# Two-layer hybrid decoder trunk on one core: the SBUF tiles of the matmul operands are given other addresses

## The chip, the core and the metric

One core of one Trainium2 chip runs the whole program in one launch. The metric is the device time of one execution in microseconds (us), from the profiler of the chip. TensorE does the matmuls, VectorE (DVE) and ScalarE (ACT) the element-wise work, GpSimd (POOL) some small vector work, and SyncE (SP) issues the DMAs. All weights are float32 and come from HBM once per execution.

## What is computed

Two layers over 256 positions with a model width of 2048. In each layer a normalised input goes through one input projection (2048 to 2816 columns), whose columns feed three mixers: sliding-window attention, a diagonal complex state-space model and a gated MLP over positions. Their outputs are normalised, concatenated and sent through an output projection (2048 to 2048). Then comes a SwiGLU feed-forward block with an inner width of 5632. Cut to the large products:

```python
for l in range(DEPTH):                       # DEPTH = 2
    h = rmsnorm(x, norm_mix[l])
    z = h @ w_in[l]                          # 256x2048 @ 2048x2816
    q, k, v, u_ssm, z_u, z_v = split(z)
    y = concat([rmsnorm(sliding_window_gqa(q, k, v)),
                rmsnorm(s5_mixer(u_ssm)),    # has one 512x512 product inside
                rmsnorm(gmlp_mixer(z_u, z_v))])
    x = x + y @ w_out[l]                     # 256x2048 @ 2048x2048
    h = rmsnorm(x, norm_ffn[l])
    x = x + (silu(h @ w_gate[l]) * (h @ w_up[l])) @ w_down[l]   # 2048x5632 twice, 5632x2048
return rmsnorm(x, norm_final)
```

## The kernel before

**Split products.** A float32 product is made of three products of a faster float32 form (float32r): each operand is split into a rounded high part and the low rest, and high times high, high times low and low times high are summed in PSUM. The function `unit` (L254 to L262) issues them: for one block of 128 input channels `k` and for each of the two halves `m` of the 256 positions, L260 multiplies the high activations with `whi`, L261 the high activations with `wlo`, and L262 the low activations with `whi`. The activations are the stationary operand (128 x 128, loaded into the array before each matmul), and the weights are the moving operand (128 x 512, streamed through). So each matmul has its own weight load, and the stationary operand changes place twice in each group of three.

**Stationary tiles.** `xh` and `xl` hold the transposed, normalised residual stream, high and low part: 16 blocks of 256 columns each. They serve the input projection and the gate and up products. `ya` and `yb` serve the output projection and the down product: `ya` holds blocks 0 to 7 (first high, then low part), `yb` blocks 8 to 15. In the profile a matmul is named by its moving and its stationary tile, in this order: `acc<-whi,xh`.

**Moving tiles.** The weights come in "halves" of 128 x 1024 floats, 512 KB each. `pump` (a DMA per half into one of 5 `raw` buffers), `split_hi` (ACT copies `raw` to `whi`, L168) and `split_lo` (DVE subtracts, `wlo`, L178) prepare them; `whi` and `wlo` have 4 buffers each. One half feeds 12 matmuls of 512 columns. Loads and splits run at most three halves ahead, by the fixed rules of `take_half`.

**Order.** The program order is written by hand: `dense` walks over the blocks, and after each block `tick` lets the side work (attention, state-space model, norms, transposes) issue a few instructions. Nothing in it depends on where a tile lies.

**Addresses.** Before the change there are two SBUF pools, `const` and `work`. A pool lays its tiles one behind the other, in the order of their first allocation, and the second pool begins where the first ends. `xh` and `xl` are allocated in `const` right behind `x`; all others named here are in `work`.

Of the kernel before, what the change touches and what calls it, by code (L numbers as in the profile page):

```python
# [1 line left out]

# [8 lines left out]
F32R = mybir.dt.float32r  # L11
# [107 lines left out]
class Split:  # L119
    def __init__(self, parts):  # L120
        self.parts = parts

    def _at(self, i, k0, k1):
        hi, lo, base = self.parts[k0 // 8 if len(self.parts) > 1 else 0]
        return (hi, lo)[i][:, k0 - base:k1 - base]
# [3 lines left out]

    def lo(self, k0, k1):  # L130
        return self._at(1, k0, k1)


class Builder:
# [811 lines left out]
    def build(self):  # L946
        nc = self.nc
        dr = self.dr
        cst = self.const
        W = self.work  # L950

        self.x = cst.tile([128, 2, 2048], F32, name="x")
        xh = cst.tile([128, 16, 256], F32R, name="xh")
        xl = cst.tile([128, 16, 256], F32R, name="xl")
        self.X = Split([(xh, xl, 0)])
        self.Y = Split([None, None])
        self.ident = cst.tile([128, 128], F32, name="ident")
# [50 lines left out]
        for l in range(L):  # L1008
# [53 lines left out]
            for t in out_tiles():  # L1062
# [12 lines left out]
                f = n not in accs  # L1075
# [80 lines left out]
        for m in range(2):  # L1156
            r = nrm["rs"][:, m:m + 1]
            t = self.work.tile([128, 2], F32, tag="ms", name="ms", bufs=4)
# [13 lines left out]
def build_program(shapes):  # L1172
    nc = bacc.Bacc("TRN2", target_bir_lowering=False, num_devices=1, dynamic_dma_scratch_size=1024)
    dr = {n: nc.dram_tensor(n, s, F32, kind="ExternalInput").ap() for n, s in shapes.items()}
    dr["out"] = nc.dram_tensor("out", (2, 128, D), F32, kind="ExternalOutput").ap()
    with tile.TileContext(nc) as tc:
        with tc.tile_pool(name="const", bufs=1) as cst, tc.tile_pool(name="work", bufs=1) as wrk, \
                tc.tile_pool(name="ps", bufs=1, space=bass.MemoryType.PSUM) as ps, \
                tc.tile_pool(name="dram", bufs=1, space=bass.MemoryType.DRAM) as dram:
            with tc.manual_schedule():  # L1180
                b = Builder(nc, tc, (cst, wrk, ps, dram), dr)
                b.build()
    return nc, b

# [11 lines left out]
```

## Time and profile before

| what | value |
|---|---|
| median of 3 runs | 2106.04 us (2104.9 to 2107.2) |
| the profiled execution: its own time | 2106.98 us |
| its span, first to last instruction | 2105.1 us |
| mean granted TensorE clock | 0.994 of 2.4 GHz |
| TensorE matmuls: busy, number | 2076.0 us, 99% of the span, 9728 |
| weight loads: busy | 1708.8 us, 81% |
| VectorE busy | 1213.1 us, 58% |
| ScalarE busy | 969.4 us, 46% |
| DMA | 387.98 MB, 184 GB/s on average |

The page counts an engine busy from the start to the (modelled) end of each instruction. Matmuls are pipelined: each is on record for some 390 ns and the next one starts some 230 ns after it, so the busy time of TensorE does not tell how fast it works. The distance from one start to the next does.

### The profile page before, as it was taken

To read this page: it belongs to the slowest core of one execution; us is meant where nothing else is said; L and a number is where in the kernel's file an instruction comes from. 1 tells how busy PE (TensorE), PEld (TensorE's weight loads), DVE (VectorE), ACT (ScalarE), POOL (GpSimd) and SP (SyncE) were. 2 spreads that over 40 slices of the span, in tenths; PEclk is the share of its full clock that TensorE was granted. 3 is DMA by queue.
4 is the path that set the end of the run, shared out by engine and by line. 5 is a ranking of instruction groups with operands and counts; after the bars stand their busy time and mean duration, and the time that the engine had idled before them with its cause. 6 is when DMAs were issued, how large, how long until landed. Compare 5 with 4: busy or idle time off the path is not lost.

```text
span 2105.1 us, 25614 instructions
## 1 busy us (share of the span) xinstructions
PE 2076.0 (99%) x9728; PEld 1708.8 (81%) x9728; DVE 1213.1 (58%) x1625; ACT 969.4 (46%) x1289; POOL 204.4 (10%) x196
## 2 busy tenths in 40 slices
PE   8998999999999999999999999999999999999998
PEld 7788888888888888888888888888888888888886
DVE  6998765655555555444556795554454444554445
ACT  6555554444444443344455445544443444434443
POOL 0555004031312100000000010000000000000000
PEclk9998999999999999999999999999999999999999
DMA  7433455565656565555565455555555555555554
GB/s 243 166 128 133 140 180 190 185 212 189 220 189 214 185 210 190 190 183 188 180 215 179 152 187 174 180 189 181 188 183 191 187 184 186 187 191 183 187 193 140
DMA packets 105595, 387.98 MB, mean 184 GB/s; under 512 B 12288, under 2 KB 13056, under 8 KB 104192
## 3 DMA queue, kind: packets, MB, share of 16 engines
q1 hardware_dynamic: 105472, 386.35, 54.8%
q8 instruction: 76, 1.25, 0.2%
q14 instruction: 47, 0.39, 0.1%
HBM read 375.03 MB, written 11.27 MB: 184 GB/s over the span
## 4 chain that ended last, share of the span: by engine, by line
PE 95%; DVE 3%; issue 1%; ACT 0%; DMA 0%; SPq 0%; POOLq 0%; POOL 0%; ACTq 0%
PE acc L260 29%; PE acc L261 29%; PE acc L262 29%; PE side L324 2%; PE side L834 1%; DVE wlo L178 1%; PE side L606 1%; PE side L798 1%; DVE st L614 0%; PE side L566 0%; PE side L823 0%; PE side L644 0%; PE side L642 0%; PE side L639 0%; DMA x<-x 0%
## 5 line engine op out<-in xcount | busy, mean ns | idle before, releaser
L178 DVE TENSOR_TENSOR wlo<-raw,whi 128x1024 fp32r<-128x1024 f32 (+1 forms) x687 | 857.5, 1253 | 686.9 <-ACT whi L168 685.7
L168 ACT ACTIVATE whi<-raw 128x1024 fp32r<-128x1024 f32 (+1 forms) x687 | 725.3, 1057 | 1005.5 <-PE acc L262 943.8
L260 PE MATMUL acc<-whi,xh 128*128 128x512 f32 (+1 forms) x1792 | 711.4, 397 | 1.4 <-ACT whi L168 1.4
L261 PE MATMUL acc<-wlo,xh 128*128 128x512 f32 (+1 forms) x1792 | 701.6, 392 | 0.2 <-DVE wlo L178 0.2
L262 PE MATMUL acc<-whi,xl 128*128 128x512 f32 (+1 forms) x1792 | 701.3, 391 | 0.0
L262 PEld LDWEIGHTS acc<-whi,xl 128*128 128x128 f32 x1792 | 337.5, 188 | 77.4
L260 PEld LDWEIGHTS acc<-whi,xh 128*128 128x128 f32 x1792 | 337.9, 189 | 73.5 <-ACT whi L168 1.8
L261 PEld LDWEIGHTS acc<-wlo,xh 128*128 128x128 f32 x1792 | 338.0, 189 | 73.0 <-DVE wlo L178 1.0
L260 PE MATMUL acc<-whi,ya 128*128 128x512 f32 x512 | 204.6, 400 | 0.0
L262 PE MATMUL acc<-whi,ya 128*128 128x512 f32 x512 | 202.0, 395 | 0.0
L261 PE MATMUL acc<-wlo,ya 128*128 128x512 f32 x512 | 202.0, 394 | 0.0
L260 PE MATMUL acc<-whi,yb 128*128 128x512 f32 x448 | 176.6, 394 | 0.0
L262 PE MATMUL acc<-whi,yb 128*128 128x512 f32 x448 | 174.8, 390 | 0.0
L261 PE MATMUL acc<-wlo,yb 128*128 128x512 f32 x448 | 174.5, 390 | 0.0
L298 POOL TENSOR_TENSOR rs<-ms,nh 128x2 f32<-128x2 f32 (+1 forms) x12 | 12.2, 1014 | 1532.9 <-DVE ms L297 1413.6
L262 PEld LDWEIGHTS acc<-whi,ya 128*128 128x128 f32 x512 | 96.3, 188 | 22.7
L261 PEld LDWEIGHTS acc<-wlo,ya 128*128 128x128 f32 x512 | 96.5, 189 | 21.5
L260 PEld LDWEIGHTS acc<-whi,ya 128*128 128x128 f32 x512 | 96.5, 189 | 21.3
L262 PEld LDWEIGHTS acc<-whi,yb 128*128 128x128 f32 x448 | 84.1, 188 | 18.0
L260 PEld LDWEIGHTS acc<-whi,yb 128*128 128x128 f32 x448 | 84.1, 188 | 17.1
L261 PEld LDWEIGHTS acc<-wlo,yb 128*128 128x128 f32 x448 | 84.2, 188 | 17.0
L360 DVE SCALAR_TENSOR_TENSOR xl<-side,gains,xh 128x256 fp32r<-128x256 f32 x64 | 27.9, 479 | 45.6 <-ACT xh L358 45.5
(223 smaller groups left out, 1278.0 us busy)
## 6 DMA issues: line engine op xcount, KB each, us to landing
raw<-wts SPq DMA_DIRECT2D x684, 512.0 KB, 3.8
saved<-stash SPq DMA_DIRECT2D x4, 1792.0 KB, 6.5
stash<-saved SPq DMA_DIRECT2D x3, 1792.0 KB, 7.4
stashb<-saved SPq DMA_DIRECT2D x2, 1792.0 KB, 9.4
bc<-bc SPq DMA_DIRECT2D x8, 256.0 KB, 3.5
out<-x SPq DMA_DIRECT2D x8, 256.0 KB, 3.0
saved<-stashb SPq DMA_DIRECT2D x1, 1792.0 KB, 7.4
x<-x SPq DMA_DIRECT2D x3, 512.0 KB, 8.0
```

Of the source, the lines that this page charges most:

```text
L168: self.nc.scalar.activation(out=h[:, o:o + w], in_=self.raw[j][:, o:o + w], func=AF.Copy)
L178: self.nc.vector.tensor_tensor(out=o[:, i:i + w], in0=r[:, i:i + w], in1=self.hi[j][:, i:i + w], op=ALU.subtract)
L260: nc.tensor.matmul(out=o, lhsT=a, rhs=wh, start=first, stop=False)
L261: nc.tensor.matmul(out=o, lhsT=a, rhs=wl, start=False, stop=False)
L262: nc.tensor.matmul(out=o, lhsT=b, rhs=wh, start=False, stop=last)
L298: nc.gpsimd.tensor_tensor(out=out, in0=t, in1=self.nh[:, 0:w], op=ALU.pow)
L324: nc.tensor.transpose(ps[:, 256 * kk + 128 * m:256 * kk + 128 * m + 128], parts(2 * b + kk, m), self.ident)
L360: nc.vector.scalar_tensor_tensor(out=o, in0=src, scalar=gain[:, k:k + 1], in1=h.bitcast(F32), op0=ALU.mult, op1=ALU.subtract)
L606: nc.tensor.matmul(out=ps[:, 256 * o + 64 * g:256 * o + 64 * g + 64], lhsT=st[nm][:, 128 * g:128 * g + 128], rhs=U4[:, 4 * ct + g, :])
L798: nc.tensor.matmul(out=ps[:, nk * i:nk * i + nk], lhsT=qT[:, h0 + i], rhs=self.kT[:, j, cq, 0:nk], start=(j == 0), stop=(j == 1))
L834: nc.tensor.matmul(out=ps[:, 64 * i:64 * i + 64], lhsT=pT[:, 128 * (nb * i + b):128 * (nb * i + b) + 128], rhs=self.v[:, b, 64 * cq:64 * c ...
```

## The change

`xh` and `xl` move from the pool `const` into the class `Homes`, which stands in place of the one pool `work`. It holds three pools, one behind the other in SBUF, and sends each tag to one of them: tags that are named nowhere to the first, `whi`, `wlo`, `xh` and `xl` to the second, `ya` and `yb` to the third. Numbers and sizes of the buffers stay as they are. On each engine the same instructions stand in the same order with the same waits; only addresses differ.

```diff
+class Homes:
+    TAGS = (
+        (),
+        ('whi', 'wlo', 'xh', 'xl'),
+        ('ya', 'yb'),
+    )
+    def __init__(self, pools):
+        self.home = {t: p for ts, p in zip(self.TAGS, pools) for t in ts}
+        self.rest = pools[0]
+    def tile(self, shape, dtype, tag, name, bufs=1):
+        return self.home.get(tag, self.rest).tile(shape, dtype, tag=tag, name=name, bufs=bufs)
...
-        xh = cst.tile([128, 16, 256], F32R, name="xh")
-        xl = cst.tile([128, 16, 256], F32R, name="xl")
+        xh = W.tile([128, 16, 256], F32R, tag="xh", name="xh")
+        xl = W.tile([128, 16, 256], F32R, tag="xl", name="xl")
...
-        with tc.tile_pool(name="const", bufs=1) as cst, tc.tile_pool(name="work", bufs=1) as wrk, \
...
+            cst = pool("const")
+            homes = Homes([pool(f"work{i}") for i in range(len(Homes.TAGS))])
...
-                b = Builder(nc, tc, (cst, wrk, ps, dram), dr)
+                b = Builder(nc, tc, (cst, homes, ps, dram), dr)
```

Where the tiles lie in each partition, in KiB from the start of SBUF (from the two built programs):

| tile | size | before | after |
|---|---|---|---|
| `x` (residual stream, float32) | 16 | 1.125 to 17.125 | 1.125 to 17.125 |
| `xh`, `xl` (stationary) | 16 each | 17.125 to 49.125 | 127.75 to 159.75 |
| `raw`, 5 buffers | 20 | 56.625 to 76.625 | 24.625 to 44.625 |
| `whi`, 4 buffers (moving) | 16 | 78.75 to 94.75 | 159.75 to 175.75 |
| `wlo`, 4 buffers (moving) | 16 | 94.75 to 110.75 | 175.75 to 191.75 |
| `t4`, 4 buffers (side work) | 16 | 110.75 to 126.75 | 46.75 to 62.75 |
| `qT`, `kT` (attention) | 8, 4 | 134.875 to 142.875, 143.875 to 147.875 | 70.875 to 78.875, 79.875 to 83.875 |
| `yb` (stationary) | 16 | 148.0 to 164.0 | 191.75 to 207.75 |
| `ya` (stationary) | 16 | 197.375 to 213.375 | 207.75 to 223.75 |

## Rows read from the trace of the kernel before

**Rows 1.** The page: span, then busy time, share and instructions by engine

```profile
span 2105.1 us, 25614 instructions
PE 2076.0 (99%) x9728; PEld 1708.8 (81%) x9728; DVE 1213.1 (58%) x1625; ACT 969.4 (46%) x1289; POOL 204.4 (10%) x196
```

**Rows 2.** The page: chain that ended last, shares of the span by engine

```profile
PE 95%; DVE 3%; issue 1%; ACT 0%; DMA 0%; SPq 0%; POOLq 0%; POOL 0%; ACTq 0%
```

**Rows 3.** Waits of TensorE: waiting line, releaser, total us, times, longest us

```profile
PE side L324 <- DMA x<-x: 6.7, 2, 4.6
PE side L834 <- DVE pT L829: 5.9, 4, 2.3
...
PE acc L260 <- ACT whi L168: 1.4, 1, 1.4
```

**Rows 4.** Groups by form: moving,stationary, shape, count | busy us, mean ns | idle

```profile
L260 PE MATMUL acc<-whi,xh 128*128 128x512 f32 x1728 | 693.1, 401 | 1.4 <-ACT whi L168 1.4
L261 PE MATMUL acc<-wlo,xh 128*128 128x512 f32 x1728 | 683.5, 396 | 0.2 <-DVE wlo L178 0.2
L262 PE MATMUL acc<-whi,xl 128*128 128x512 f32 x1728 | 683.2, 395 | 0.0
L260 PE MATMUL acc<-whi,ya 128*128 128x512 f32 x512 | 204.6, 400 | 0.0
L262 PE MATMUL acc<-whi,ya 128*128 128x512 f32 x512 | 202.0, 395 | 0.0
L261 PE MATMUL acc<-wlo,ya 128*128 128x512 f32 x512 | 202.0, 394 | 0.0
L260 PE MATMUL acc<-whi,yb 128*128 128x512 f32 x448 | 176.6, 394 | 0.0
L262 PE MATMUL acc<-whi,yb 128*128 128x512 f32 x448 | 174.8, 390 | 0.0
L261 PE MATMUL acc<-wlo,yb 128*128 128x512 f32 x448 | 174.5, 390 | 0.0
```

**Rows 5.** Timeline, down product of layer 2: start us, duration us, instruction; yb, then ya

```profile
1838.24 0.39 PE L261 MATMUL acc<-wlo,yb 128*128 128x512 f32 x1
...
1847.76 0.39 PE L261 MATMUL acc<-wlo,yb 128*128 128x512 f32 x1
...
1848.22 0.40 PE L260 MATMUL acc<-whi,ya 128*128 128x512 f32 x1
...
1859.14 0.40 PE L262 MATMUL acc<-whi,ya 128*128 128x512 f32 x1
```

**Rows 6.** Timeline, gate and up products of layer 1

```profile
1000.15 0.39 PE L261 MATMUL acc<-wlo,xh 128*128 128x512 f32 x1
...
1008.09 0.39 PE L262 MATMUL acc<-whi,xl 128*128 128x512 f32 x1
```

**Rows 7.** Groups by form: the matmuls of 256 columns, main and attention

```profile
L260 PE MATMUL acc<-whi,xh 128*128 128x256 f32 x64 | 18.3, 286 | 0.0
L262 PE MATMUL acc<-whi,xl 128*128 128x256 f32 x64 | 18.1, 283 | 0.0
L261 PE MATMUL acc<-wlo,xh 128*128 128x256 f32 x64 | 18.1, 282 | 0.0
...
L798 PE MATMUL side<-kT,qT 128*128 128x256 f32 x64 | 10.4, 290 | 0.0
```

**Rows 8.** Windows: stretch, busy us (count) by engine, clock, DMA share, GB/s

```profile
0.00:200.00 200.00, 180.19 (x1022) 153.74 (x1022) 169.09 (x377) 119.99 (x232) 81.41 (x88) 0.98 0.51 175
...
1470.00:2105.00 635.00, 625.80 (x2737) 507.57 (x2735) 313.37 (x295) 258.96 (x273) 1.79 (x2) 1.00 0.55 183
```

**Rows 9.** The page: the two splits of a weight half, and its DMA

```profile
L178 DVE TENSOR_TENSOR wlo<-raw,whi 128x1024 fp32r<-128x1024 f32 (+1 forms) x687 | 857.5, 1253 | 686.9 <-ACT whi L168 685.7
L168 ACT ACTIVATE whi<-raw 128x1024 fp32r<-128x1024 f32 (+1 forms) x687 | 725.3, 1057 | 1005.5 <-PE acc L262 943.8
...
raw<-wts SPq DMA_DIRECT2D x684, 512.0 KB, 3.8
```

More of the change, by code (lines that the diff above doesn't have):

```diff
@@ L1 @@
+import contextlib
 import math
@@ L1176, in build_program @@
     with tile.TileContext(nc) as tc:
-        with tc.tile_pool(name="const", bufs=1) as cst, tc.tile_pool(name="work", bufs=1) as wrk, \
-                tc.tile_pool(name="ps", bufs=1, space=bass.MemoryType.PSUM) as ps, \
-                tc.tile_pool(name="dram", bufs=1, space=bass.MemoryType.DRAM) as dram:
+        with contextlib.ExitStack() as st:
+            pool = lambda name, **kw: st.enter_context(tc.tile_pool(name=name, bufs=1, **kw))
+            cst = pool("const")
+            homes = Homes([pool(f"work{i}") for i in range(len(Homes.TAGS))])
+            ps = pool("ps", space=bass.MemoryType.PSUM)
+            dram = pool("dram", space=bass.MemoryType.DRAM)
             with tc.manual_schedule():
-                b = Builder(nc, tc, (cst, wrk, ps, dram), dr)
+                b = Builder(nc, tc, (cst, homes, ps, dram), dr)
                 b.build()
```

## The prediction, made before the changed kernel ran

> **What bounds the kernel now.** I read the page from the top first: TensorE is busy for 99% of the span [rows 1] and carries 95% of the chain that ended last [rows 2]. The waits of TensorE come to little: the longest entry is 6.7 us at the start, and the splits of the weights hold it up for about 1.4 us [rows 3]. So nobody feeds TensorE late; what counts is how fast it gets through its own matmuls. A change of addresses alone can touch the time only there, or by making another engine slow enough to be waited for.
>
> The second view is the timeline, read by distances between starts. With `yb` as stationary tile, 42 matmuls in a row take 1847.76 - 1838.24 = 9.52 us, which is 226.7 ns each; with `ya`, in the same down product right behind it, 47 take 1859.14 - 1848.22 = 10.92 us, 232.3 ns each [rows 5]. With `xh` and `xl`, 34 take 1008.09 - 1000.15 = 7.94 us, 233.5 ns each [rows 6]. All three stretches have the same shape, the same moving buffers, the granted clock at the 2.4 GHz level, and no waits. At that clock 512 columns need 213.3 ns if one column goes in per cycle, so every matmul pays 13 to 20 ns on top, and how much depends on which stationary tile it has.
>
> The third view, the groups by form, shows that this isn't a chance of three stretches. Over all matmuls of 512 columns the mean durations are 401, 396 and 395 ns for `xh`, `xh` and `xl` at L260, L261 and L262, 400, 394 and 395 ns for `ya`, and 394, 390 and 390 ns for `yb` [rows 4]. The differences, 7, 6 and 5 ns between `xh`/`xl` and `yb`, are those of the timeline. What the three tiles differ in is the address: `xh` and `xl` lie between 17 and 49 KiB, `ya` between 197 and 213, `yb` between 148 and 164, and `whi` and `wlo` always between 79 and 111.
>
> **The change part by part.** No instruction is added, removed or moved, and no queue is passed; the sum has only paces in it.
>
> *Residual tiles.* `xh` and `xl` go to 127.75 to 159.75 KiB, almost on the place where `yb` was. I give them its pace: 1728 x (401 - 394) + 1728 x (396 - 390) + 1728 x (395 - 390) ns = 12.1 + 10.4 + 8.6 = 31.1 us less [rows 4]. The other bound is 0, if the place was not what made `yb` fast. The 192 matmuls of 256 columns I leave at 0: they are 0.2 us per ns.
>
> *Branch tiles.* `yb` goes to 191.75 to 207.75 KiB, where `ya` was for most of that stretch. I give it `ya`'s pace: 448 x (6 + 5 + 4) ns = 6.7 us more, and 0.2 us for its 48 further matmuls in the state-space branch, so 6.9 us more [rows 4]. The other bound is 0. `ya` stays at the top and keeps its pace; its other bound is `yb`'s pace, 512 x (6 + 5 + 4) ns = 7.7 us less.
>
> *Weight tiles.* `whi` and `wlo` go from 79-111 to 160-192 KiB. The trace has no dense matmul with its moving tile elsewhere, so this cost is unknown on both sides. The only matmuls of some length with both operands between 128 and 192 KiB are those of attention, `kT` with `qT`, 256 columns: 290 ns on average, against 282 to 286 for the main matmuls of the same shape [rows 7]. The 290 also has pauses between heads in it. So the nearest row shows neither a gain nor a clear loss, and I take 0. For the bounds I use one more step of the size that the trace does show, 6 ns per matmul either way: over 3 x (1728 + 512 + 448) + 48 = 8112 matmuls that is 49 us.
>
> *Splits, transposes and DMAs* read and write other addresses too. Their cost is taken as 0, since TensorE covers them: a half feeds 12 matmuls, 12 x 233 ns = 2.80 us, in which DVE needs 1.25 us and ACT 1.06 us for it [rows 9], and at 12 x 227 ns = 2.72 us that still fits. The DMA engines are busy for 0.55 of the last stretch and would be for 0.57 [rows 8]. The cover is thinnest in the first 200 us, where DVE is busy for 169 us [rows 8]: if the whole gain were lost there, it would be at most 1022 x 6 ns = 6 us, which goes into the range.
>
> The sum is -31.1 + 6.9 = -24.2 us. The profiled execution took 2106.98 us, 0.9 above the median of the runs and 1.9 above its own span, so both are one state; 2106.98 - 24.2 = 2082.8, and from the median 2106.04 the forecast is 2082 us.
>
> **The rivals.**
>
> *Alignment, not region.* `yb` starts at 148.0 KiB, a multiple of 256 bytes; `xh` at 17.125 and `ya` at 197.375 KiB are both 128 bytes off one. Each stationary block is 512 bytes long in its partition, so it touches two pieces of 256 bytes if aligned and three if not, and the extra 13.3 and 20 ns stand just as 2 to 3. In the new layout all four tiles begin at such a multiple. Then `xh`, `xl` and `ya` all get `yb`'s pace and `yb` keeps it: -31.1 - 7.7 = -38.8, about 2067 us. Against it: the attention tile `qT` is 128 bytes off too, and its matmuls show no special price [rows 7].
>
> *The moving place counts as well, in the good direction.* One more step of 6 ns for all: -49 on the forecast, about 2033 us. Nothing in the trace shows a main matmul below 226 ns.
>
> *Place is irrelevant.* The paces may belong to the stage and not to the tile; then nothing changes, 2106 us. Against it: `ya` and `yb` differ within one and the same down product, with the same side work around [rows 5]. The Trainium skill speaks for this case: "TensorE: Matmul & The Clock Gate", in its step-by-step part, has the two operands on independent SBUF read ports, so that a weight load takes no bandwidth from the running matmul, and it gives some 216 ns from start to start at 512 columns. "SBUF — State Buffer", under who interferes with whom, says that TensorE never waits for anyone there. The trace differs from these pages: 226.7, 232.3 and 233.5 ns.
>
> *The pace belongs to the pair (slower).* `yb` may have been fast since it lay in another 64 KiB range than its moving tile and at the right distance from it, and not by its own place. The change puts `xh` and `xl` beside `whi` and `wlo` in one range, so they stay at 233 ns, and `yb` loses its distance: +6.9, 2113 us. It is slower as soon as less than 6.9 of the 31.1 us of the residual tiles come.
>
> *Both operands collide in one range (slower).* If a weight load and a stream out of the same 64 KiB hinder each other more than now, each `xh` and `xl` matmul grows by a further step of 6 ns, 5184 x 6 = 31 us, `ya`, next to them, by 9, and `yb` by 2 steps, 17: +57, about 2163 us. For it is only the 290 against 283 ns of [rows 7].
>
> **How the numbers follow.** Chances: forecast 0.34; alignment 0.20; moving place good 0.09; irrelevant 0.12; pair 0.15; collision 0.10. The predicted time is the forecast's, 2082. The range from 2062 to 2116 holds forecast, alignment, irrelevant and pair with 2 to 5 us around, 0.81 together; it leaves out the two unknown extremes, 2033 and 2163. A measurement of this kernel can tell about 0.2%, 4 us, from no change. Faster: 0.34 + 0.20 + 0.09 = 0.63. Same: 0.12. Slower: 0.15 + 0.10 = 0.25.
>
> **What would show it.** In the trace of after, the groups `acc<-whi,xh`, `acc<-wlo,xh` and `acc<-whi,xl` should show means of 394, 390 and 390 ns, and a stretch of the timeline 227 ns from start to start. The `yb` groups should go up to 400, 394 and 395; if they stay at 394, 390 and 390 and `ya` comes down to them, it is alignment. Means below 390 would say that the moving place counts. `xh` at 401 with `yb` at 400 is the pair, and `xh` above 405 the collision. DVE and ACT means of 1253 and 1057 ns should stay, and TensorE's waits should stay below 25 us in all; waits for `whi` or `wlo` that grow by 10 us or more would make the sum wrong in a way that none of the cases holds.

## The result, and the profile after

The changed kernel takes 2071.38 us (2070.53 to 2073.31, 4 runs) against 2106.27 us for the kernel before, measured beside it. The ratio is 0.9836, with a 95% interval from 0.9819 to 0.9853: 34.9 us less. The forecast was 2082 us, 24 less, from 2062 to 2116. The sign and the range held, but the forecast gave the gain to a wrong cause, charged `yb` with a loss that did not come and missed the gain of `ya`, as the rows show.

The page of the changed kernel, the lines that answer to [rows 1] and [rows 2]:

```profile
span 2068.7 us, 25614 instructions
PE 2040.8 (99%) x9728; PEld 1707.3 (83%) x9728; DVE 1210.8 (59%) x1625; ACT 969.7 (47%) x1289; POOL 207.0 (10%) x196
...
PE 95%; DVE 3%; issue 1%; ACT 0%; DMA 0%; SPq 0%; POOLq 0%; POOL 0%; ACTq 0%
```

TensorE bounds the kernel as before, with the same instructions. Its busy time fell by 35.2 us, the span by 36.4; VectorE and ScalarE do their work in the same time (1210.8 and 969.7 us, before 1213.1 and 969.4). So it is the matmuls that got faster. Which of them, the groups by form tell (line, moving and stationary tile, shape, count, then busy us and the mean ns of one; the line numbers are 18 higher than before):

```profile
L278 PE MATMUL acc<-whi,xh 128*128 128x512 f32 x1728 | 685.7, 397 | 1.8 <-ACT whi L186 1.8
L280 PE MATMUL acc<-whi,xl 128*128 128x512 f32 x1728 | 675.5, 391 | 0.0
L279 PE MATMUL acc<-wlo,xh 128*128 128x512 f32 x1728 | 674.9, 391 | 0.4 <-DVE wlo L196 0.4
L278 PE MATMUL acc<-whi,ya 128*128 128x512 f32 x512 | 202.0, 394 | 0.0
L280 PE MATMUL acc<-whi,ya 128*128 128x512 f32 x512 | 199.6, 390 | 0.0
L279 PE MATMUL acc<-wlo,ya 128*128 128x512 f32 x512 | 199.4, 389 | 0.0
L278 PE MATMUL acc<-whi,yb 128*128 128x512 f32 x448 | 176.4, 394 | 0.0
L280 PE MATMUL acc<-whi,yb 128*128 128x512 f32 x448 | 174.6, 390 | 0.0
L279 PE MATMUL acc<-wlo,yb 128*128 128x512 f32 x448 | 174.4, 389 | 0.0
```

Against [rows 4]: `xh` and `xl` came down by 4 to 5 ns, `ya` came down by 5 to 6 ns to the values of `yb`, and `yb` did not go up at all. The timeline says the same in distances between starts, at a granted clock of 1.00 in all these stretches, before and after. First `xh` and `xl` (34 matmuls in 990.39 - 982.68 = 7.71 us, 226.8 ns each, before 233.5 [rows 6]), then `yb` (47 in 10.66 us, 226.8 ns, before 226.7) and `ya` (44 in 9.98 us, 226.8 ns, before 232.3 [rows 5]) in the down product of layer 2:

```profile
982.68 0.39 PE L279 MATMUL acc<-wlo,xh 128*128 128x512 f32 x1
...
990.39 0.39 PE L280 MATMUL acc<-whi,xl 128*128 128x512 f32 x1
...
1806.08 0.39 PE L278 MATMUL acc<-whi,yb 128*128 128x512 f32 x1
...
1816.74 0.39 PE L280 MATMUL acc<-whi,yb 128*128 128x512 f32 x1
1816.96 0.39 PE L278 MATMUL acc<-whi,ya 128*128 128x512 f32 x1
...
1826.94 0.39 PE L280 MATMUL acc<-whi,ya 128*128 128x512 f32 x1
```

All three stretches now have one pace. Over the whole trace, the distances from each start to the next, added up by stationary tile, fell by 26.7 us for `xh` and `xl`, by 8.1 us for `ya` and by 0.6 us for `yb`; 1.0 us of the 36.4 is left for everything else. The prediction said what that would mean: "if they stay at 394, 390 and 390 and `ya` comes down to them, it is alignment". The experiments had to tell which alignment, and whether the 64 KiB ranges (SBUF counted from its start in pieces of 64 KiB) had any share in it.

### The profile page after: what moved, and what is told of

It reads as the page before. It is cut to its first block, busy times and chain, and to the rows that moved or that the text cites. A ratio compares the mean times of both kernels' runs of the same rounds, so it can differ in the third digit from the quotient of the medians.

```text
span 2068.7 us, 25614 instructions
## 1 busy us (share of the span) xinstructions
PE 2040.8 (99%) x9728; PEld 1707.3 (83%) x9728; DVE 1210.8 (59%) x1625; ACT 969.7 (47%) x1289; POOL 207.0 (10%) x196
## 4 chain that ended last, share of the span: by engine, by line
PE 95%; DVE 3%; issue 1%; ACT 0%; DMA 0%; SPq 0%; POOLq 0%; POOL 0%; ACTq 0%
PE acc L278 29%; PE acc L280 29%; PE acc L279 29%; PE side L342 2%; PE side L852 1%; DVE wlo L196 1%; PE side L624 1%; PE side L816 1%; DVE st L632 0%; PE side L584 0%; PE side L841 0%; PE side L662 0%; PE side L660 0%; PE side L657 0%; DMA raw<-wts 0%
## 5 line engine op out<-in xcount | busy, mean ns | idle before, releaser
L196 DVE TENSOR_TENSOR wlo<-raw,whi 128x1024 fp32r<-128x1024 f32 (+1 forms) x687 | 855.2, 1250 | 659.7 <-ACT whi L186 658.9
L186 ACT ACTIVATE whi<-raw 128x1024 fp32r<-128x1024 f32 (+1 forms) x687 | 726.0, 1058 | 972.2 <-PE acc L280 920.8
L278 PE MATMUL acc<-whi,xh 128*128 128x512 f32 (+1 forms) x1792 | 704.0, 393 | 1.8 <-ACT whi L186 1.8
L280 PE MATMUL acc<-whi,xl 128*128 128x512 f32 (+1 forms) x1792 | 693.6, 387 | 0.0
L279 PE MATMUL acc<-wlo,xh 128*128 128x512 f32 (+1 forms) x1792 | 693.0, 387 | 0.4 <-DVE wlo L196 0.4
L280 PEld LDWEIGHTS acc<-whi,xl 128*128 128x128 f32 x1792 | 337.6, 188 | 69.4
L278 PE MATMUL acc<-whi,ya 128*128 128x512 f32 x512 | 202.0, 394 | 0.0
L280 PE MATMUL acc<-whi,ya 128*128 128x512 f32 x512 | 199.6, 390 | 0.0
L280 PE MATMUL acc<-whi,yb 128*128 128x512 f32 x448 | 174.6, 390 | 0.0
L280 PEld LDWEIGHTS acc<-whi,ya 128*128 128x128 f32 x512 | 96.1, 188 | 20.3
L280 PEld LDWEIGHTS acc<-whi,yb 128*128 128x128 f32 x448 | 84.1, 188 | 17.7
```

The lines of the kernel that those rows point to most:

```text
L186: self.nc.scalar.activation(out=h[:, o:o + w], in_=self.raw[j][:, o:o + w], func=AF.Copy)
L196: self.nc.vector.tensor_tensor(out=o[:, i:i + w], in0=r[:, i:i + w], in1=self.hi[j][:, i:i + w], op=ALU.subtract)
L278: nc.tensor.matmul(out=o, lhsT=a, rhs=wh, start=first, stop=False)
L279: nc.tensor.matmul(out=o, lhsT=a, rhs=wl, start=False, stop=False)
L280: nc.tensor.matmul(out=o, lhsT=b, rhs=wh, start=False, stop=last)
```

## The experiments

Three theories were open. **Alignment**: the stationary tile has to begin at a multiple of 256 bytes. **Relative alignment**: it has to be a multiple of 256 bytes away from the moving tile, wherever both are; two tiles at such a distance are called in step below. **Region pair**: 64 KiB ranges count, and a stationary tile is fast in the range of its moving tile or in the next one above; all the places seen so far fit that too. The first four runs were made in one job, beside 2105.26 us for the kernel before. In the profiles of the runs the line numbers are higher by the lines that an edit adds.

### 128 unused bytes ahead of `xh`, in the kernel before

```diff
         self.x = cst.tile([128, 2, 2048], F32, name="x")
+        cst.tile([128, 32], F32, name="pad")
         xh = cst.tile([128, 16, 256], F32R, name="xh")
```

> The kernel before with one unused tile of 128 bytes allocated ahead of xh, and nothing else: every tile behind it moves up by 128 bytes and stays in its old place otherwise (xh 17.25, whi 78.875, yb 148.125, ya 197.5 KiB). Theory alignment (the stationary tile has to begin at a multiple of 256 bytes): xh, xl and ya become aligned and yb falls out of line, so xh, xl and ya come down to 394/390/390 ns and yb goes up to 400/395/394: -29 to -31 -8 +7, about 2075 us. Rival region pair (fast when the stationary tile lies in the same 64 KiB range as the moving one or in the next above): no range changes, 2106 us and the means of before. Rival relative alignment (the distance from stationary to moving tile counts modulo 256 bytes): all tiles move together, 2106 us.

Measured: 2105.96 us, ratio 1.0002 (0.9992 to 1.0011). The groups kept their means; one of each kind:

```profile
L260 PE MATMUL acc<-whi,xh 128*128 128x512 f32 x1728 | 693.1, 401 | 1.4 <-ACT whi L168 1.4
...
L261 PE MATMUL acc<-wlo,ya 128*128 128x512 f32 x512 | 202.0, 394 | 0.0
...
L261 PE MATMUL acc<-wlo,yb 128*128 128x512 f32 x448 | 174.6, 390 | 0.0
```

`xh`, `xl` and `ya` now begin at multiples of 256 bytes and are as slow as before, and `yb` lies 128 bytes off one and is as fast as before. So the tile's own alignment does not count; the alignment rival, as the prediction put it, has fallen. Since everything moved together, the distances did not change.

### 128 unused bytes at the start of the second pool, in the changed kernel

```diff
-        ('whi', 'wlo', 'xh', 'xl'),
+        ('whi', 'wlo', 'xh', 'xl', 'pad', 'pad2'),
...
+        W.tile([128, 32], F32, tag="pad", name="pad")
         xh = W.tile([128, 16, 256], F32R, tag="xh", name="xh")
```

> The changed kernel with an unused tile of 128 bytes at the start of the second pool: xh, xl, whi, wlo, yb and ya all move up by 128 bytes, each in its 64 KiB range. Theory alignment: all stationary tiles fall out of line, 400/395/394 ns for xh, xl, ya and yb, and the time goes back beyond the kernel before: 2071 + 30 + 8 + 7, about 2116 us (2106 if the step is a little smaller than measured). Rival region pair: 2071 us. Rival relative alignment: 2071 us, since stationary and moving tiles move together.

Measured: 2071.42 us, ratio 0.9839 (0.9823 to 0.9856), the changed kernel's own time. It is the counterpart of the first run: all operands are off a multiple of 256 bytes, all distances are as they were, and nothing is lost.

### Only `xh` and `xl` 128 bytes off

```diff
-        ('whi', 'wlo', 'xh', 'xl'),
         ('ya', 'yb'),
+        ('whi', 'wlo'),
+        ('pad', 'xh', 'xl'),
...
+        W.tile([128, 32], F32, tag="pad", name="pad")
         xh = W.tile([128, 16, 256], F32R, tag="xh", name="xh")
```

> The changed kernel with the three groups in another order: ya and yb from 127.75, whi and wlo from 159.75 (where the change puts them), then 128 unused bytes, then xh and xl from 191.875 KiB. Only xh and xl are off a multiple of 256 bytes. Theory alignment: xh and xl at 400/395/394 ns, ya and yb at 394/390/390, 2071 + 30 = about 2101 us. Rival region pair: ya and yb share the range of whi and wlo, xh and xl lie in the next above, so all are fast: 2071 us. Rival relative alignment: as alignment, 2101 us.

Measured: 2097.13 us, ratio 0.9963 (0.9950 to 0.9976), 25.7 us more than the 2071.42 of the run before it, in which all distances are those of the changed kernel. The groups at the first two lines of the three:

```profile
L279 PE MATMUL acc<-whi,xh 128*128 128x512 f32 x1728 | 693.7, 401 | 1.5 <-ACT whi L187 1.5
L280 PE MATMUL acc<-wlo,xh 128*128 128x512 f32 x1728 | 683.6, 396 | 0.6 <-DVE wlo L197 0.6
...
L279 PE MATMUL acc<-whi,ya 128*128 128x512 f32 x512 | 202.0, 395 | 0.0
...
L280 PE MATMUL acc<-wlo,yb 128*128 128x512 f32 x448 | 174.4, 389 | 0.0
```

Exactly the two tiles that are out of step went back to 401 and 396 ns. The region pair has fallen with this: `xh` lies between 192 and 208 KiB with its moving tile between 160 and 192, just where `yb` was fast in the changed kernel, and differs from it by 128 bytes.

### Only `whi` and `wlo` 128 bytes off

```diff
-        ('whi', 'wlo', 'xh', 'xl'),
         ('ya', 'yb'),
+        ('xh', 'xl'),
+        ('pad', 'whi', 'wlo'),
```

(and the same unused tile as above)

> The changed kernel with ya and yb from 127.75, xh and xl from 159.75, then 128 unused bytes, then whi and wlo from 191.875 KiB: only the moving tiles are off a multiple of 256 bytes, and all stationary ones are aligned. Theory alignment of the stationary tile: nothing changes, 2071 us and 394/390/390 ns in all groups. Rival relative alignment: all matmuls slow, about 2116 us. Rival region pair: all stationary tiles lie one range below the moving ones, as xh and xl did before, so all slow: about 2116 us.

Measured: 2114.83 us, ratio 1.0044 (1.0029 to 1.0058). Every stationary tile begins at a multiple of 256 bytes, and every group is slow, `yb` with them. `xh` and `xl` lie at 159.75 to 191.75 KiB here, inside the region from 128 to 192 KiB that the forecast took for fast:

```profile
L279 PE MATMUL acc<-whi,xh 128*128 128x512 f32 x1728 | 693.4, 401 | 1.8 <-ACT whi L187 1.8
...
L280 PE MATMUL acc<-wlo,ya 128*128 128x512 f32 x512 | 202.1, 395 | 0.0
...
L280 PE MATMUL acc<-wlo,yb 128*128 128x512 f32 x448 | 176.9, 395 | 0.0
```

So the same loss comes from moving the other operand. Of the three theories only the relative one fits all four runs.

### 128 unused bytes ahead of `whi`, in the kernel before

A second job (before: 2104.69 us) turned the theory into an edit of the old layout that should help with no tile leaving its range.

```diff
+        if not j:
+            self.work.tile([128, 32], F32, tag="pad", name="pad")
         h = self.work.tile([128, 1024], F32R, tag="whi", name="whi", bufs=self.NH)
```

> The kernel before with 128 unused bytes ahead of whi (the first run put them ahead of xh). xh and xl stay at 17.125 KiB, whi moves to 78.875, yb to 148.125, ya to 197.5 KiB. Theory relative alignment (the matmul is fast when stationary and moving tile are a multiple of 256 bytes apart): xh and xl come into step (61.75 KiB apart) and fall to about 396/391/391 ns, yb stays in step (69.25) at 394/390/390, ya stays out of step (118.625) at 400/395/394: 2105 - 29 = about 2076 us. Rival region pair, or any theory of 64 KiB ranges: no tile changes its range, 2105 us.

Measured: 2079.42 us, ratio 0.9879 (0.9863 to 0.9896), 25.3 us less from 128 bytes that nothing uses.

```profile
L262 PE MATMUL acc<-whi,xh 128*128 128x512 f32 x1728 | 684.7, 396 | 2.2 <-ACT whi L170 2.2
...
L263 PE MATMUL acc<-wlo,ya 128*128 128x512 f32 x512 | 201.9, 394 | 0.0
...
L263 PE MATMUL acc<-wlo,yb 128*128 128x512 f32 x448 | 174.6, 390 | 0.0
```

`xh` came into step (397 or less), `yb` stayed in step and `ya` out of it, each as expected. The first run put the same 128 bytes ahead of `xh`, where they moved both operands, and got nothing.

### Distances of 32 to 224 bytes

Two variants of the changed kernel put `whi` and `wlo` first and unused tiles of 32 to 160 bytes ahead of the stationary tiles (only the order of the tags and the sizes of these tiles differ).

> The changed kernel with whi and wlo first (127.75 KiB), then xh and xl 32 bytes, yb 64 bytes and ya 96 bytes beyond a multiple of 256 from them. Theory pieces of 256 bytes, all or nothing: every distance that isn't 0 costs the full step, all groups at 400/395/394 ns, about 2114 us. Rival graded cost: the step grows from 0 to 128 bytes, so xh and xl lose little (1 to 3 ns, below 2085 us in all), yb about half, ya more. Rival steps of 128 or 64 bytes: groups below the boundary stay at 394/390/390.

> The same with xh and xl 160 bytes, yb 192 and ya 224 bytes beyond a multiple of 256 from whi. All or nothing: all groups at 400/395/394 ns, about 2114 us. Graded: ya nearly at 394/390/390, yb half way, xh and xl most. Steps of 128 bytes: all as at 128, slow; steps of 64: ya differs from the others.

Measured: 2115.89 and 2113.46 us, one run each. One group of each tile, first with `xh` 32, `ya` 96 and `yb` 64 bytes out of step:

```profile
L281 PE MATMUL acc<-wlo,xh 128*128 128x512 f32 x1728 | 684.8, 396 | 0.2 <-DVE wlo L198 0.2
...
L281 PE MATMUL acc<-wlo,ya 128*128 128x512 f32 x512 | 202.9, 396 | 0.0
...
L281 PE MATMUL acc<-wlo,yb 128*128 128x512 f32 x448 | 177.0, 395 | 0.0
```

and then with `xh` 160, `ya` 224 and `yb` 192 bytes out of step:

```profile
L281 PE MATMUL acc<-wlo,xh 128*128 128x512 f32 x1728 | 687.1, 398 | 0.6 <-DVE wlo L198 0.6
...
L281 PE MATMUL acc<-wlo,ya 128*128 128x512 f32 x512 | 202.1, 395 | 0.0
...
L281 PE MATMUL acc<-wlo,yb 128*128 128x512 f32 x448 | 176.9, 395 | 0.0
```

At 390 they would be fast (391 for `xh`). By these means it is all or nothing: of the distances tried in steps of 32 bytes, only the multiples of 256 are fast, and 32 bytes cost as much as 128. Each of these distances was tried with one stationary tile (`xh` and `xl` together) and in one run.

The starts in the second of these traces show one exception. `yb`, 192 bytes out of step, took 9.38 us for 41 matmuls in the output projection of layer 1, 228.8 ns each, and 10.97 us for 47 in the down product of layer 2, 233.4 ns each, both at a granted clock of 1.00:

```profile
247.86 0.39 PE L280 MATMUL acc<-whi,yb 128*128 128x512 f32 x1
...
257.24 0.39 PE L282 MATMUL acc<-whi,yb 128*128 128x512 f32 x1
...
1841.87 0.40 PE L280 MATMUL acc<-whi,yb 128*128 128x512 f32 x1
...
1852.84 0.40 PE L282 MATMUL acc<-whi,yb 128*128 128x512 f32 x1
```

So at this distance most of the loss is absent in one stretch and all of it there in another. The trace has the lower pace in both output projections and in parts of layer 1's down product, and no run tells why.

### Only `xl` 128 bytes off

```diff
-        ('whi', 'wlo', 'xh', 'xl'),
         ('ya', 'yb'),
+        ('whi', 'wlo'),
+        ('xh', 'pad', 'xl'),
...
         xh = W.tile([128, 16, 256], F32R, tag="xh", name="xh")
+        W.tile([128, 32], F32, tag="pad", name="pad")
         xl = W.tile([128, 16, 256], F32R, tag="xl", name="xl")
```

> The changed kernel with ya, yb, whi, wlo and xh in step (127.75 to 207.75 KiB) and xl alone 128 bytes off. Theory that the running matmul is held up by the weight load for the next one: xl is loaded while the wlo,xh matmul runs, so wlo,xh (396 ns) grows and whi,xl and whi,xh stay near 390 and 395. Theory that a matmul is held up by its own stationary tile: whi,xl grows to 395. Either way a third of the residual tiles' 29 us is lost: about 2081 us; if one swap out of step puts the whole train out of step, more, up to 2100.

Measured: 2091.09 us (one run), between the two simple answers. The groups and, in the timeline, one round of the three matmuls and the starts of the second and the fourth:

```profile
L281 PE MATMUL acc<-whi,xl 128*128 128x512 f32 x1728 | 686.6, 397 | 0.0
L280 PE MATMUL acc<-wlo,xh 128*128 128x512 f32 x1728 | 685.1, 396 | 0.6 <-DVE wlo L197 0.6
L279 PE MATMUL acc<-whi,xh 128*128 128x512 f32 x1728 | 685.1, 396 | 1.4 <-ACT whi L187 1.4
```

```profile
990.09 0.39 PE L279 MATMUL acc<-whi,xh 128*128 128x512 f32 x1
990.31 0.40 PE L280 MATMUL acc<-wlo,xh 128*128 128x512 f32 x1
990.55 0.40 PE L281 MATMUL acc<-whi,xl 128*128 128x512 f32 x1
990.78 0.39 PE L279 MATMUL acc<-whi,xh 128*128 128x512 f32 x1
...
992.17 0.39 PE L279 MATMUL acc<-whi,xh 128*128 128x512 f32 x1
```

`wlo,xh` at L280, during which `xl` is loaded for the next matmul, went from 391 to 396 ns; so did `whi,xl` at L281, which has `xl` in the array, from 391 to 397. `whi,xh`, which has nothing to do with `xl`, kept its 396 (397 in the changed kernel). From start to start the nine matmuls of three rounds take 992.17 - 990.09 = 2.08 us, 231.1 ns each, between 226.8 in step and 233.5 out of it. Two matmuls of three pay, and 2 x 1728 x 5.5 ns = 19 us is about what this one run lost against the changed kernel (2091.09 - 2071.38 = 19.7). Neither the theory of the next load alone nor that of the own tile alone gives that.

### The kernel before with all tiles in step

A third job compared the old layout, put in step, with the changed kernel (before: 2105.54 us). Beside the 128 bytes ahead of `whi` it has 128 ahead of `ya`, and to make room the two smallest tiles of the gated MLP become one:

```diff
+            if ct == 1 and not hasattr(self, "pad2"):
+                self.pad2 = self.work.tile([128, 32], F32, tag="pad2", name="pad2")
             t = self.work.tile([128, 4096], F32, tag=("ya", "yb")[ct - 1], name="stashb", bufs=1)
...
-        mv = self.work.tile([128, 2, 2], F32, tag="mv", name="mv", bufs=1)
-        rv = self.work.tile([128, 2], F32, tag="rv", name="rv", bufs=1)
+        mvr = self.work.tile([128, 3, 2], F32, tag="mv", name="mv", bufs=1)
+        mv, rv = mvr[:, 0:2], mvr[:, 2]
```

> The kernel before with 128 unused bytes ahead of whi and 128 ahead of ya (and the two smallest tiles of the gated MLP put into one, to make room): every tile stays in its old 64 KiB range, and xh, xl, yb and ya are all multiples of 256 bytes from whi. Theory relative alignment: all groups at the pace of the changed kernel, 227 ns from start to start, about 2071 us, the same as the changed kernel in the same job. Rival that the new ranges have a share of their own in the gain: it stays behind the changed kernel by that share (5 us or more would be seen).

> The changed kernel itself, for comparison in the same job: 2071 us.

Measured: 2071.56 us (ratio 0.9836, 0.9820 to 0.9852) and 2070.64 us (0.9834, 0.9820 to 0.9849). The groups of the old layout in step:

```profile
L262 PE MATMUL acc<-whi,xh 128*128 128x512 f32 x1728 | 685.7, 397 | 1.4 <-ACT whi L170 1.4
...
L263 PE MATMUL acc<-wlo,ya 128*128 128x512 f32 x512 | 199.6, 390 | 0.1
...
L263 PE MATMUL acc<-wlo,yb 128*128 128x512 f32 x448 | 174.6, 390 | 0.0
```

These are the means of the changed kernel, within 1 ns. Two pieces of 128 bytes give the whole gain, and the new 64 KiB ranges have no share in it that can be measured. No run was faster than the changed kernel.

## Why the prediction was right and where it was wrong

**What bounds the kernel: right.** The reading that a change of addresses can only work through TensorE's own pace, and that the pace goes with the tile's place and not with the stage, was confirmed: TensorE's 35.2 us less of busy time is the gain, and the rival that place is irrelevant has fallen with every run that moved one operand by 128 bytes and not the other.

**Cause: wrong.** The forecast took the region from 128 to 192 KiB for what made `yb` fast. But `xh` and `xl` were slow inside that region (401 and 396 ns, `whi` and `wlo` put off) and fast at their old place outside it (396 and 390 ns, 128 bytes ahead of `whi`). What counted for `yb` was its distance from `whi`, 148.0 - 78.75 = 69.25 KiB, a multiple of 256 bytes, while `xh` was at -61.625 and `ya` at 118.625 KiB. In the new layout these tiles, all multiples of 4 KiB long, stand one behind another without a gap, so that every distance among them is a multiple of 256 bytes. The rows could have told more than was taken from them: the prediction worked out the remainder by 256 bytes for the stationary tiles but not for `whi`, and looked at the stationary tile alone. That the sum still fell into the range was luck: `xh` and `xl` came down because the new layout happens to put them in step, and the range was wide enough for the rest since it was drawn to hold other rivals too.

**Residual tiles, -31.1 us: the sign was right, the term too large.** Alone they measured -25.3 us (128 bytes ahead of `whi`) and +25.7 us (`xh` and `xl` put off). The step that failed is taking the whole difference of group means, 7, 6 and 5 ns, as theirs. In step, `xh` and `xl` stay at 397, 391 and 391 ns, 1 to 3 above `yb`, so a part of the difference in [rows 4] was not a matter of place.

**Branch tiles, +6.9 us: wrong, for both tiles.** `yb` lost nothing, and `ya` gained; the value was taken from the tile that had lain nearest to the new place, and near in KiB was no measure. In step against out of step `ya` is worth some 8 us (2079.42 and 2071.56 us for the two old layouts, with `ya` out and in, and 8.1 us by the distances between starts), close to the 7.7 us named as its other bound. With -25.5 and -8 the sum is -33.5; measured -34.9, so 1.4 us are in neither.

**Weight tiles, 0: right for the place, but the step taken as their bound was real in another way.** Put 128 bytes off they slow down every main matmul (2114.83 us, 43.4 more than the 2071.42 with the same distances as in the changed kernel; the bound was 49).

**Rivals.** Alignment came nearest, 2067 us against 2071, and had the tiles right; its condition was wrong, as the first two runs show. The argument against it, that `qT` is 128 bytes off and pays nothing, was none: by the table of addresses `kT` and `qT` begin 9 KiB apart, in step with each other, and at their 256 columns no step was seen in any tile. The pair rival had the right thought, that the two operands count together, but in ranges of 64 KiB, and so forecast a loss. Nothing was seen of the collision, and nothing of a moving place that is good by itself: `whi` and `wlo` moved by 81 KiB, and `yb` kept 226.7 to 226.8 ns.

**Splits and DMAs, 0: right.** VectorE and ScalarE show 1250 and 1058 ns for their splits (before 1253 and 1057), and TensorE still waits little:

```profile
PE side L852 <- DVE pT L847: 5.5, 3, 3.2
PE side L342 <- DMA x<-x: 5.2, 2, 4.6
...
PE acc L278 <- ACT whi L186: 1.8, 1, 1.8
```

## What to carry to other kernels

Where TensorE is busy all the time and each matmul has its own stationary tile, look at the distance from start to start by stationary tile: here, two paces at one shape, one clock and one stage were a matter of addresses. Then look at the distance in bytes between the two operands' tiles; a few unused bytes are quickly tried, and a layout that is rearranged for another reason can win or lose this step by accident. When several tiles move at once, change one distance at a time before believing in regions.

## What the runs showed of the hardware

With a float32r moving operand of 128 x 512 and a weight load for each matmul, at the 2.4 GHz level (granted clock 1.00 in the stretches read), the start-to-start distance was some 227 to 229 ns in stretches of 23 matmuls or more where the two tiles were a multiple of 256 bytes apart in their partitions (226.7 to 226.8 in those shown), and some 232 to 234 ns at the other distances tried (32, 64, 96, 128, 160, 192 and 224 bytes beyond such a multiple), but for the 229 ns of `yb` at 192 bytes in a part of its stretches. The absolute addresses and the 64 KiB ranges made no difference. The Trainium skill ("SBUF — State Buffer", Who interferes with whom) says that TensorE never waits on anyone there. In these runs the place of TensorE's own two operands to each other cost it 5 to 7 ns per matmul; that their two reads delay each other would fit, but no run shows it.

The effect was not seen in the main matmuls of 256 columns. `xh` and `xl` came into step for these as well, and their means are 287, 283 and 283 ns after [rows 7]:

```profile
L278 PE MATMUL acc<-whi,xh 128*128 128x256 f32 x64 | 18.4, 287 | 0.0
L280 PE MATMUL acc<-whi,xl 128*128 128x256 f32 x64 | 18.1, 283 | 0.0
L279 PE MATMUL acc<-wlo,xh 128*128 128x256 f32 x64 | 18.1, 283 | 0.0
```

What stays open: why the distance counts, whether the load of the next tile or the tile in the array sets it (the matmul that runs while `xl` is loaded and the one that uses it both paid), why 192 bytes cost little in some stretches, why 256 columns don't pay, and what the 13 ns are that even the matmuls in step take beyond the 213.3 ns that 512 columns need at 2.4 GHz if one goes in per cycle. In no layout did a stretch go below 226.6 ns.
